# An encoder layer on one core: another order of loads and products at the beginning, another ending of the last norm

## The chip, the core and the metric

The kernel runs on one core of one Trainium2 chip. A core has a matrix engine (TensorE, PE in the profile, with its weight loads shown apart as PEld), a vector engine (VectorE, DVE), an activation engine (ScalarE, ACT), a general engine (GpSimd, POOL) and an engine that does little but issue transfers (SyncE, SP). Each works through its own list of instructions in order; semaphores tie the lists together. Data moves between the main memory and the core's own memory (128 partitions) in DMA transfers, which an engine issues and 16 DMA engines carry out. The metric is the device time of one execution in microseconds, the median over runs; lower is better.

## The reference

One layer of an encoder over 256 positions of width 2048, all in float32. Each of its three parts is normed before and after, and added to the running X:

```python
ff = swiglu(rms_norm(x, pre_norm_ffn1[layer]), w_ffn1_gate_up[layer], w_ffn1_down[layer])
x = x + 0.5 * rms_norm(ff, post_norm_ffn1[layer])
h = rms_norm(x, pre_norm_mix[layer])
...
x = x + rms_norm(mixed, post_norm_mix[layer])
ff = swiglu(rms_norm(x, pre_norm_ffn2[layer]), w_ffn2_gate_up[layer], w_ffn2_down[layer])
x = x + 0.5 * rms_norm(ff, post_norm_ffn2[layer])
```

`rms_norm` divides a row by the root of its mean square plus 1e-6 and multiplies by a gain. `swiglu` multiplies by a gate-and-up matrix of 2048 x 11264, takes silu of the gate half times the up half, and multiplies by a down matrix of 5632 x 2048. The change touches only the first products of the first `swiglu` and the last two lines of arithmetic of the whole layer.

## The kernel before

**Precision.** A float32 product is made of three products of a faster format: each operand is split into a high part `h` and a rest `l`, and `three` (L435) adds `xh*h`, `xh*l` and `xl*h` into a bank of PSUM, the matrix engine's accumulators. For weights, `split_act` (L175) makes the parts: ACT copies raw weights into `h` (a cast, L176), then DVE subtracts (`l`, L177). For X, PE transposes blocks of 128 x 128 into a bank (`turn`, L205; the operation itself is L210), ACT scales them by the norm's gain into the high part (`take_hi`, L224, L227), and DVE makes the rest (`take_lo`, L229, L232). The norm's own factor is applied later.

**Tiles.** X stands as two row tiles (m = 0, 1) of 128 rows. Its 2048 columns are 16 blocks of 128 (index k of the products), or four quarters q of 512. The gate-and-up matrix is worked in groups of 512 columns of gate and 512 of up (n = 0, 1), so a group has four banks (m, n). A pair u is two blocks of 128 rows of the weights, so a pair's raw tile holds four parts of 256 KB (k = 0, 1; n = 0, 1) and gives 24 products into the four banks. `gated.piece(u, k, m)` (L969) is six of them.

**The beginning** (L96 to L135 and L1241 to L1317). SP issues the loads in program order: first the norm's gains as 16 rows (in `to_columns`, L109, which turns them into columns with one transpose and a DVE copy), then X's first quarter of row tile 0 (`load_x`, L92, L94), the first quarter of pair 0's weights (`arrive`, L1257), X's first quarter of row tile 1, three more parts of pair 0, the second quarters of X, pair 1, the rest of X in two loads, pair 2. `busy(n)` (L126) issues n products of zeros into an unused bank; they stand in PE's list five after the start, two after the gains, three after the first transposes. Then the order is written out by hand, engine by engine (`tc.manual_schedule`, L1244): each engine carries out what stands in the code in the order in which it stands there. `half(i)` splits a part of pair 0, `taken` is the scaling and rest of transposed blocks, `square_x` (L246) is ACT's sum of squares of a quarter of X for the norm, and `split` (L158) splits the two halves of a pair's weights, ACT's cast and DVE's subtract for each half. Behind line 1317 come pairs 3 to 7 of the group, with an order that the framework chooses.

**The end** (`finish`, L686, the branch from L732). The last two pairs of the down matrix are held back, and their products are ordered bank by bank: (0,0), (0,1), (1,0), (1,1). After each bank ACT takes the sum of squares (`squares`, L712; L667), one of four columns per row tile. After a tile's second bank, `rsqrt_of` (L180) adds the four columns (L182, DVE), scales and adds eps (L184, DVE), and raises to the power -1/2 (L186, POOL). Then DVE updates X by quarters (`update`, L719, L721), the first quarter of row tile 1 goes over ACT (L727) and POOL (L728) (`update_aside`), and SP stores each quarter (`store`, L733, L735), the one that POOL makes last.

## Time and profile before

| | us |
|---|---|
| median of 3 runs | 1833.32 (1832.61 to 1833.54) |
| the profiled execution's own time | 1832.88 |
| its span, first to last instruction | 1831.1 |
| PE busy in the span | 1814.2 |
| DVE busy | 1627.3 |
| ACT busy | 1129.4 |

The granted clock was 0.997 on average. In the profile, L with a number is a line of the kernel, `out<-in` names the tiles written and read, and an arrow in brackets names what ended an engine's idle time. A timeline's row gives start and duration in us; rows that follow one another with the same form are merged, with their count after the x. In a table of windows each row gives a stretch, its length, and for each engine the busy time with the number of instructions, then the granted clock, the share of the DMA engines' time that is busy, and GB/s. Rows with "min/median/max" give durations in ns, and "DMA to landing" the us from a transfer's issue until its data has arrived.

### The profile page before, as it was taken

What the parts mean: (1) busy time and instruction counts of PE and PEld (TensorE: products, weight loads), DVE (VectorE), ACT (ScalarE), POOL (GpSimd) and SP (SyncE); (2) the same over time, 40 slices, a digit from 0 to 9 for tenths busy, and PEclk for the clock granted to TensorE, in tenths of its full rate; (3) what the DMA queues carried; (4) which work ended last, traced back from release to release, by engine and by line L of the source; (5) the groups of instructions that cost most, each with busy time, mean ns of one, the idle gap of its engine ahead of it and who ended that gap; (6) DMA issues with size and microseconds to landing.
All of it is one profiled execution on the core that took longest, in us unless ns stands there. A gap on an engine that the chain in (4) does not pass through costs nothing.

```text
span 1831.1 us, 23305 instructions
## 1 busy us (share of the span) xinstructions
PE 1814.2 (99%) x8438; PEld 1504.0 (82%) x8438; DVE 1627.3 (89%) x2071; ACT 1129.4 (62%) x1492; POOL 114.4 (6%) x115
## 2 busy tenths in 40 slices
PE   9999999999999999999999999999999999999998
PEld 6888888888887888888888888788888888888886
DVE  7999999999999998477787798899999999999897
ACT  7565666665655666476587556556666666565563
POOL 1011111111000000000000000001111111000000
PEclk9999999999999999999999999999999999999999
DMA  8789999998665566555454456789998998855565
GB/s 301 230 234 283 278 280 253 251 266 241 249 226 197 195 253 216 203 175 178 165 173 150 161 208 249 223 243 267 280 277 267 252 251 251 268 218 207 193 231 185
DMA packets 200020, 422.42 MB, mean 231 GB/s; under 512 B 10984, under 2 KB 45888, under 8 KB 199136
## 3 DMA queue, kind: packets, MB, share of 16 engines
q1 hardware_dynamic: 178880, 380.95, 59.6%
q0 software_dynamic: 21024, 39.99, 12.7%
q8 instruction: 66, 1.08, 0.2%
q14 instruction: 50, 0.41, 0.1%
HBM read 408.29 MB, written 12.60 MB: 230 GB/s over the span
## 4 chain that ended last, share of the span: by engine, by line
PE 87%; DVE 5%; ACT 3%; DMA 3%; issue 2%; POOL 0%; SPq 0%; DVEq 0%; ACTq 0%; POOLq 0%
PE pa L441 37%; PE pb L441 33%; PE pa L309 5%; DVE l L177 3%; PE pa L314 3%; DMA raw<-in_w_ffn_gate_up_dram 2%; PE pa L364 2%; PE pa L362 2%; PE pa L363 2%; ACT h L176 1%; PE pa L1074 1%; PE pb L1074 1%; PE pb L1582 0%; PE pb L1556 0%; PE pb L1660 0%
## 5 line engine op out<-in xcount | busy, mean ns | idle before, releaser
L176 ACT CAST h<-raw 128x1024 fp32r<-128x1024 f32 (+1 forms) x861 | 846.9, 1013 | 448.6 <-PE pb L441 131.9
L177 DVE TENSOR_TENSOR l<-raw,h 128x1024 fp32r<-128x1024 f32 (+1 forms) x861 | 983.1, 1171 | 118.3 <-ACT h L176 83.8
L441 PE MATMUL pa<-h,xt 128*128 128x512 f32 x1104 | 387.2, 392 | 0.1
L441 PE MATMUL pb<-h,xt 128*128 128x512 f32 x952 | 339.7, 391 | 0.4 <-DVE pb L1126 0.4
L441 PEld LDWEIGHTS pa<-h,xt 128*128 128x128 f32 x1104 | 207.2, 188 | 43.9 <-DVE xt L232 0.6
L441 PE MATMUL pa<-l,xt 128*128 128x512 f32 x552 | 215.7, 391 | 0.2 <-DVE l L177 0.2
L441 PEld LDWEIGHTS pb<-h,xt 128*128 128x128 f32 x952 | 178.6, 188 | 43.2 <-DVE pb L1133 3.5
L441 PE MATMUL pb<-l,xt 128*128 128x512 f32 x476 | 185.6, 390 | 0.0
L441 PE MATMUL pb<-h,ht 128*128 128x512 f32 x464 | 163.8, 390 | 0.0
L441 PE MATMUL pa<-h,ht 128*128 128x512 f32 x464 | 163.7, 391 | 0.0
L910 POOL DMA_DIRECT2D raw<-in_w_ffn_gate_up_dram x76 | 92.0, 1211 | 737.0 <-DVE l L177 638.8
L309 PE MATMUL pa<-xt,h 128*128 128x512 f32 x512 | 124.5, 393 | 0.2 <-ACT h L176 0.2
L441 PEld LDWEIGHTS pa<-l,xt 128*128 128x128 f32 x552 | 103.7, 188 | 21.4 <-DVE l L177 1.4
L309 PEld LDWEIGHTS pa<-xt,h 128*128 128x128 f32 x512 | 93.8, 188 | 18.6 <-ACT h L176 0.6
L441 PE MATMUL pa<-h,xs 128*128 128x512 f32 x304 | 108.5, 389 | 0.0
L441 PE MATMUL pb<-h,xs 128*128 128x512 f32 x304 | 105.9, 389 | 0.0
L441 PEld LDWEIGHTS pb<-l,xt 128*128 128x128 f32 x476 | 89.4, 188 | 17.2
L441 PEld LDWEIGHTS pa<-h,ht 128*128 128x128 f32 x464 | 87.7, 189 | 18.4
L441 PEld LDWEIGHTS pb<-h,ht 128*128 128x128 f32 x464 | 87.3, 188 | 18.1
L441 PE MATMUL pa<-l,ht 128*128 128x512 f32 x232 | 90.9, 392 | 0.0
L441 PE MATMUL pb<-l,ht 128*128 128x512 f32 x232 | 90.5, 390 | 0.0
L314 PE MATMUL pa<-xt,l 128*128 128x256 f32 x512 | 69.1, 285 | 0.0
(289 smaller groups left out, 2516.9 us busy)
## 6 DMA issues: line engine op xcount, KB each, us to landing
raw<-in_w_ffn_gate_up_dram SPq DMA_DIRECT2D x350, 512.0 KB, 6.1
raw<-in_w_ffn_down_dram SPq DMA_DIRECT2D x88, 1024.0 KB, 5.3
raw<-in_w_mix_in_dram SPq DMA_DIRECT2D x52, 1024.0 KB, 4.9
raw<-in_w_ffn_gate_up_dram POOLq DMA_DIRECT2D x76, 512.0 KB, 8.8
raw<-in_w_mix_out_dram SPq DMA_DIRECT2D x16, 1024.0 KB, 5.0
away<-ht SPq DMA_DIRECT2D x16, 512.0 KB, 6.9
ht<-away SPq DMA_DIRECT2D x16, 512.0 KB, 7.8
pg<-in_post_norm_ffn_dram SPq DMA_DIRECT2D x4, 512.0 KB, 6.7
```

The lines of the kernel that those rows point to most:

```text
L176: nc.scalar.copy(hi, src)
L177: nc.vector.tensor_tensor(lo, src, hi.bitcast(F32), ALU.subtract)
L309: nc.tensor.matmul(slot[f], weights(hs, kk, f), xcol(xt, k), start=(k == 0), stop=(k == KT - 1))
L314: nc.tensor.matmul(slot[f][:, 0:T], weights(ls, kk, f), xcol(xt, kh * 8 + kk, 0), start=False, stop=False,)
L362: nc.tensor.matmul(dst, xh, h[:, o : o + n], start=(k == 0), stop=False)
L363: nc.tensor.matmul(dst, xh, l[:, o : o + n], start=False, stop=False)
L364: nc.tensor.matmul(dst, xl, h[:, o : o + n], start=False, stop=(k == KT - 1))
L441: nc.tensor.matmul(self.bank(at), lhs, rhs, start=(n == 1), stop=n in (ends, self.of[at]), skip_group_check=n > ends,)
L910: nc.gpsimd.dma_start(raw[:, 0:1024].rearrange("p (k c) -> p k c", k=2), self.source(u, g)[:, :, 1], accum_op=ALU.add,)
L1074: nc.tensor.transpose(bank[:, o : o + P], zs[m][:, k * P : (k + 1) * P], ident)
```

## The change

At the beginning, X's first quarter is loaded in three parts (one block, one block, two blocks of 128 columns) for each row tile; the very first block is the first thing that SP issues. The gains and the first block of row tile 1 are issued from ACT. The second weight part is loaded ahead of X's next blocks, and X's other quarters follow pair 1 and pair 2 instead of standing ahead of them. `turn` can now transpose single blocks into a bank that is already in use. Pair 0's products are made block by block, and within a block the products with the weights' rest come last. The idle products are five, two and two. Transposes of blocks 1, 2 and 3 stand between pair 0's products, and those of the second quarter between the halves of pair 1. Each engine's list follows the new order, as before.

At the end, the first three of row tile 1's square sums are added, scaled and joined with eps on DVE while the last bank's products run (`rsqrt_most`), and the fourth is scaled and added afterwards (`rsqrt_rest`), in place of a reduction over four. The last store is issued from ACT.

```diff
@@ -89,10 +89,15 @@
 
     res = {"X": new_X()}
 
-    def load_x(m, q, n=1):
-        sl = slice(q * 512, (q + n) * 512)
-        nc.sync.dma_start(res["X"][:, m, sl], x[0, m * P : (m + 1) * P, sl])
-
+    def load_x(m, a, b, queue=nc.sync):
+        sl = slice(a * P, b * P)
+        queue.dma_start(res["X"][:, m, sl], x[0, m * P : (m + 1) * P, sl])
+
+    load_x(0, 0, 1)
+    stat = ctx.enter_context(tc.tile_pool(name="stat", bufs=4))
+    gain_rows = stat.tile([P, P], F32, tag="dg", name=nm("rows"), bufs=1)
+    nc.scalar.dma_start(gain_rows[:KT, :], pre_norm_ffn1[0].rearrange("(j p) -> j p", p=P))
+    load_x(1, 0, 1, nc.scalar)
     warm = const.tile([P, 4], F32, tag="warm", name="warm")
     nc.vector.memset(warm, 0.0)
     nc.scalar.activation(warm, warm, AF.Silu)
@@ -102,14 +107,15 @@
     nc.vector.memset(ones, 1.0)
     mhalf = const.tile([P, 4], F32, tag="mhalf", name="mhalf")
     nc.vector.memset(mhalf, -0.5)
-    stat = ctx.enter_context(tc.tile_pool(name="stat", bufs=4))
-
     stat.tile([P, 104], F32, tag="line", name="line", bufs=1)
 
-    def to_columns(srcs, tag, eng):
-
-        rows = stat.tile([P, P], F32, tag="dg", name=nm("rows"), bufs=1)
+    def to_columns(srcs, tag, eng, rows=None):
+
         r0 = 0
+        if rows is not None:
+            r0, srcs = srcs, ()
+        else:
+            rows = stat.tile([P, P], F32, tag="dg", name=nm("rows"), bufs=1)
         for src in srcs:
             n = src.shape[0] // P
             eng.dma_start(rows[r0 : r0 + n, :], src.rearrange("(j p) -> j p", p=P))
@@ -130,9 +136,7 @@
             nc.tensor.matmul(bank, idle[:, 0:P], idle, start=(i == 0), stop=(i == n - 1))
 
     busy(5)
-    gain1 = to_columns([pre_norm_ffn1[0]], "gain1", nc.sync)
-    load_x(0, 0)
-    busy(2)
+    gain1 = to_columns(KT, "gain1", None, gain_rows)
 
     R = const.tile([P, T], F32, tag="R", name="R")
     scales = const.tile([P, 8], F32, tag="scales", name="scales")
@@ -186,6 +190,19 @@
         nc.gpsimd.tensor_tensor(r, v, mhalf[:, 0:1], ALU.pow)
         return r
 
+    def rsqrt_most(ssq, scale, eps):
+        tot = stat.tile([P, 1], F32, tag="tot", name=nm("tot"))
+        nc.vector.tensor_reduce(tot, ssq, axis=AX.X, op=ALU.add)
+        nc.vector.tensor_scalar(tot, tot, scale, eps, ALU.mult, ALU.add)
+        return tot
+
+    def rsqrt_rest(ssq, scale, most):
+        v = stat.tile([P, 1], F32, tag="v", name=nm("v"))
+        nc.vector.tensor_scalar(v, ssq, scale, most, ALU.mult, ALU.add)
+        r = stat.tile([P, 1], F32, tag="r", name=nm("r"))
+        nc.gpsimd.tensor_tensor(r, v, mhalf[:, 0:1], ALU.pow)
+        return r
+
     far = {}
     shim = ctx.enter_context(tc.tile_pool(name="shim", bufs=1, side="right"))
     shim.tile([P, 104], F32, tag="shim", name="shim")
@@ -202,10 +219,10 @@
         open_far(2)
         return [far["pool"].tile([P, 8, 2, T], F32R, tag="xt", name=nm("xt")) for _ in range(2)]
 
-    def turn(m, q):
-
-        bank = pa() if m == 0 else pb()
-        for j in range(4):
+    def turn(m, q, bank=None, js=range(4)):
+
+        bank = bank or (pa() if m == 0 else pb())
+        for j in js:
             k = q * 4 + j
             nc.tensor.transpose(
                 bank[:, j * P : (j + 1) * P], res["X"][:, m, k * P : (k + 1) * P], ident
@@ -434,18 +451,21 @@
 
         def three(self, at, ah, al, h, l):
             for lhs, rhs in ((ah, h), (ah, l), (al, h)):
-                n = self.seen.get(at, 0) + 1
-                self.seen[at] = n
-
-                ends = self.of[at] - (self.rest if at[0] == "c" else 0)
-                nc.tensor.matmul(
-                    self.bank(at),
-                    lhs,
-                    rhs,
-                    start=(n == 1),
-                    stop=n in (ends, self.of[at]),
-                    skip_group_check=n > ends,
-                )
+                self.one(at, lhs, rhs)
+
+        def one(self, at, lhs, rhs):
+            n = self.seen.get(at, 0) + 1
+            self.seen[at] = n
+
+            ends = self.of[at] - (self.rest if at[0] == "c" else 0)
+            nc.tensor.matmul(
+                self.bank(at),
+                lhs,
+                rhs,
+                start=(n == 1),
+                stop=n in (ends, self.of[at]),
+                skip_group_check=n > ends,
+            )
 
         def plain(self, u, hs, ls, m, n, k):
             a = self.tiles[u]
@@ -700,7 +720,7 @@
             X = res["X"]
             if lead:
                 lead.load()
-            r = [None, None]
+            r, most = [None, None], [None, None]
             y = self.y
 
             def products(m, n, part):
@@ -711,8 +731,15 @@
 
             def squares(m, n):
                 self.squares(m, n)
-                if n == 1:
-                    r[m] = rsqrt_of(self.ssq[m], 1.0 / (D * mul * mul), EPS / (mul * mul))
+                if n == 1 and most[m] is None:
+                    r[m] = rsqrt_of(self.ssq[m], scale, eps)
+                elif n == 1:
+                    r[m] = rsqrt_rest(self.ssq[m][:, 3:4], scale, most[m])
+
+            scale, eps = 1.0 / (D * mul * mul), EPS / (mul * mul)
+
+            def mostly(m):
+                most[m] = rsqrt_most(self.ssq[m][:, 0:3], scale, eps)
 
             gains = self.gains
 
@@ -730,9 +757,9 @@
             ordered = {mybir.EngineType.PE, mybir.EngineType.DVE, mybir.EngineType.Activation}
             every = slice(None)
             if gain is None:
-                def store(m, q):
+                def store(m, q, queue=nc.sync):
                     sl = slice(q * 512, (q + 1) * 512)
-                    nc.sync.dma_start(out[0, m * P : (m + 1) * P, sl], X[:, m, sl])
+                    queue.dma_start(out[0, m * P : (m + 1) * P, sl], X[:, m, sl])
 
                 def in_place(n):
                     gains(1, n, dst=self.c[1][n])
@@ -749,6 +776,7 @@
                     squares(1, 0)
                     for q in range(4):
                         update(0, q)
+                    mostly(1)
                     in_place(0)
                     products(1, 1, every)
                     squares(1, 1)
@@ -759,7 +787,7 @@
                     for q in (1, 2, 3):
                         update(1, q)
                         store(1, q)
-                    store(1, 0)
+                    store(1, 0, nc.scalar)
                 return None
 
             xt = new_xt()
@@ -1244,8 +1272,8 @@
     with tc.manual_schedule():
         banks = {}
 
-        def turned(*at):
-            banks[at] = turn(*at)
+        def turned(m, q, js=range(4)):
+            banks[m, q] = turn(m, q, banks.get((m, q)), js)
 
         def taken(m, q, js=range(4)):
             take(m, q, gain1, xt, banks[m, q], js)
@@ -1257,54 +1285,84 @@
         def arrive(i):
             nc.sync.dma_start(raw[:, i * 512 : (i + 1) * 512], first[:, i // 2, i % 2])
 
-        h, l = (
-            p.tile([P, 1024], F32R, tag=t, name=nm(t)) for p, t in ((hip, "h"), (lop, "l"))
+        hs, ls = zip(
+            *(
+                [p.tile([P, 1024], F32R, tag=t, name=nm(t)) for p, t in ((hip, "h"), (lop, "l"))]
+                for _ in range(2)
+            )
         )
+        gated.parts = {0: (hs, ls)}
 
         def half(i):
-            cs = slice(i * 512, (i + 1) * 512)
-            split_act(h[:, cs], l[:, cs], raw[:, cs])
-
-        def piece(m, n):
-            gated.plain(0, [h], [l], m, n, 0)
+            cs = slice(i % 2 * 512, (i % 2 + 1) * 512)
+            split_act(hs[i // 2][:, cs], ls[i // 2][:, cs], raw[:, i * 512 : (i + 1) * 512])
+
+        def piece(k, m, n, order):
+            a, ms, cs = gated.tiles[0], slice(m * P, (m + 1) * P), slice(n * 512, (n + 1) * 512)
+            terms = (0, hs), (0, ls), (1, hs)
+            for i, w in (terms[j] for j in order):
+                gated.one(("c", m, n), a[:, k, i, ms], w[k][:, cs])
+
+        def block(k, n):
+            for m in range(2):
+                piece(k, m, n, (0, 2))
+            for m in range(2):
+                piece(k, m, n, (1,))
+
+        def column(j):
+            for m in range(2):
+                turned(m, 0, [j])
+
+        def column_taken(j):
+            for m in range(2):
+                taken(m, 0, [j])
 
         arrive(0)
-        load_x(1, 0)
         arrive(1)
+        load_x(0, 1, 2)
+        load_x(1, 1, 2)
         arrive(2)
         arrive(3)
-        load_x(0, 1)
-        load_x(1, 1)
+        load_x(0, 2, 4)
+        load_x(1, 2, 4)
         raws = [load(gated.source(1))]
-        load_x(0, 2, 2)
-        load_x(1, 2, 2)
+        load_x(0, 4, 8)
+        load_x(1, 4, 8)
         raws.append(load(gated.source(2)))
-        turned(0, 0)
+        load_x(0, 8, 16)
+        load_x(1, 8, 16)
+        turned(0, 0, [0])
         taken(0, 0, [0])
-        busy(3)
         half(0)
-        taken(0, 0, [1, 2, 3])
-        turned(1, 0)
-        piece(0, 0)
+        busy(2)
+        turned(1, 0, [0])
+        busy(2)
+        piece(0, 0, 0, (0, 2))
         taken(1, 0, [0])
         half(1)
-        piece(1, 0)
-        piece(0, 1)
-        piece(1, 1)
-        hs, ls = zip((h, l), split_half(raw, 1))
-        gated.parts = {0: (hs, ls)}
-        taken(1, 0, [1, 2, 3])
-        gated.piece(0, 1, 0)
-        gated.piece(0, 1, 1)
+        piece(0, 1, 0, (0, 2))
+        for m in range(2):
+            piece(0, m, 0, (1,))
+        column(1)
+        column_taken(1)
+        block(0, 1)
+        half(2)
+        half(3)
+        block(1, 0)
+        column(2)
+        column(3)
+        block(1, 1)
+        column_taken(2)
+        column_taken(3)
         gated.parts[1] = split(raws[0])
+        for m in range(2):
+            gated.piece(1, 0, m)
+        for m in range(2):
+            turned(m, 1)
+            taken(m, 1)
         square_x(0, 0)
-        turned(0, 1)
-        turned(1, 1)
-        taken(0, 1)
-        taken(1, 1)
-        for k in range(2):
-            for m in range(2):
-                gated.piece(1, k, m)
+        for m in range(2):
+            gated.piece(1, 1, m)
         gated.parts[2] = split(raws[1])
         square_x(1, 0)
         for k in range(2):
```

## The prediction

> **What bounds the kernel now.** I read the page's first part, then the timeline of the first 30 us, then TensorE's (PE's) products by window, then the chain of waits and the DMA shares at the end.
>
> ```profile
> span 1831.1 us, 23305 instructions
> PE 1814.2 (99%) x8438; PEld 1504.0 (82%) x8438; DVE 1627.3 (89%) x2071; ACT 1129.4 (62%) x1492; POOL 114.4 (6%) x115
> ```
>
> PE is busy for all but 17 us, and from its first real product to its last it works almost without a gap. So a change of the two ends can only move where that stretch starts, what it loses on the way, and what follows its end. The start, from the timeline (start, duration, engine, line; in brackets the idle time and who ended it):
>
> ```profile
> 0.73 1.28 ACT L98 ACT_TABLE_LOAD   x1 [0.73 <-PEq L1846]
> 0.74 0.40 SPq L115 DMA_DIRECT2D rows<-in_pre_norm_ffn_dram  x1
> 1.20 0.41 SPq L94 DMA_DIRECT2D X<-in_x_dram  x1
> 1.37 2.31 PE L130 MATMUL pb<-idle 128*128 128x512 bf16 x5 [1.37 <-DVE idle L124]
> 3.94 0.17 DVE L120 COPY gain<-pb 128x16 f32<-128x16 f32 x1 [2.62 <-PE pb L119]
> 5.05 0.73 PE L210 MATMUL pa<-ident,X 128*128 128x128 f32 x4 [0.18 <-DMA X<-in_x_dram]
> 5.62 0.81 PE L130 MATMUL pb<-idle 128*128 128x512 bf16 x3
> 6.11 0.62 ACT L176 CAST h<-raw 128x512 fp32r<-128x512 f32 x1
> 6.22 0.35 DVE L232 SCALAR_TENSOR_TENSOR xt<-pa,gain,xt 128x128 fp32r<-128x128 f32 x1 [2.10 <-ACT xt L227]
> 6.76 0.69 DVE L177 TENSOR_TENSOR l<-raw,h 128x512 fp32r<-128x512 f32 x1 [0.19 <-ACT h L176]
> 6.90 0.63 PE L210 MATMUL pb<-ident,X 128*128 128x128 f32 x4 [0.47 <-DMA X<-in_x_dram]
> 7.28 0.47 PE L441 MATMUL pa<-h,xt 128*128 128x512 f32 x1
> ...
> 11.91 1.05 ACT L176 CAST h<-raw 128x1024 fp32r<-128x1024 f32 x1 [1.23 <-DMA raw<-in_w_ffn_gate_up_dram]
> 13.26 1.05 ACT L176 CAST h<-raw 128x1024 fp32r<-128x1024 f32 x1 [0.30 <-DMA raw<-in_w_ffn_gate_up_dram]
> 13.86 0.60 PE L210 MATMUL pa<-ident,X 128*128 128x128 f32 x4
> 14.22 0.62 ACT L254 ACTIVATE jk<-X 128x512 bf16<-128x512 f32 x1
> 14.84 1.12 ACT L227 ACTIVATE xt<-pa,gain 128x128 fp32r<-128x128 f32 x4
> 15.84 1.16 ACT L227 ACTIVATE xt<-pb,gain 128x128 fp32r<-128x128 f32 x4
> 18.30 1.23 DVE L177 TENSOR_TENSOR l<-raw,h 128x1024 fp32r<-128x1024 f32 x1
> ```
>
> X's first 256 KB, issued at 1.20, reach PE at 5.05; the first weight block is cast at 6.11; the second 256 KB of X let PE go on at 6.90; the first product starts at **7.28**. Later weights come at one rate: 11.91 and 13.26, two 512 KB halves 1.35 us apart, so 0.67 us for 256 KB. How smoothly PE then runs:
>
> ```profile
> core 0: us, PE busy (x) PEld busy (x), PEclk, DMA share, GB/s
> 14.65:20.19 5.54, 5.54 (x25) 4.59 (x26) 1.00 1.04 386
> 7.28:13.86 6.58, 6.34 (x24) 4.09 (x24) 1.00 1.04 397
> ```
>
> Pair 1's 24 products take 5.54 us (0.23 each, no gap); pair 0's 24 take 6.58, so waits cost **1.06 us** there. The end:
>
> ```profile
> 1823.31 0.16 DVE L182 TENSOR_REDUCE tot<-ssqr 128x1 f32<-128x4 f32 x1 [0.99 <-ACT jk L667]
> 1823.50 0.15 DVE L184 TENSOR_SCALAR v<-tot 128x1 f32<-128x1 f32 x1
> ```
> ```profile
> 1826.00:1826.50 0.50, 0.00 (x0) 0.00 (x0) 0.45 (x1) 0.00 (x0) 0.44 (x1) 0.50 0.97 369
> 1826.50:1827.00 0.50, 0.00 (x0) 0.00 (x0) 0.00 (x0) 0.00 (x0) 0.00 (x0) 0.50 1.06 385
> 1827.00:1827.50 0.50, 0.00 (x0) 0.00 (x0) 0.00 (x0) 0.00 (x0) 0.00 (x0) 0.50 1.11 361
> ```
>
> The reduction of the square sums is a 0.19 us step after the last square (1823.31 to 1823.50), and DVE stood idle for 0.99 us ahead of it. The last four stores then keep the DMA engines full (the last column but one, the DMA share, is 0.97 to 1.11).
>
> **The start, step by step.** *First product.* X's first block (64 KB) takes the issue slot at 0.74, and the first weights (256 KB) the one at 1.20 that X's 256 KB had. The startup is slow, then full:
>
> ```profile
> 4.00:4.50 0.50, 0.50 (x2) 0.00 (x0) 0.12 (x1) 0.00 (x0) 0.00 (x0) 1.00 0.20 66
> 5.00:5.50 0.50, 0.45 (x3) 0.45 (x4) 0.00 (x0) 0.00 (x0) 0.00 (x0) 1.00 1.05 402
> ```
>
> I let the weights inherit that slot's landing, 5.0. The cast (0.62) then ends at 5.65 and the first product starts at **5.70**: -1.58 us. X's side is earlier: gain is there at 4.11, transpose, scaling (0.37: four in 1.12, 0.25 apart) and residual (0.35, the row at 6.22) end near 4.95. Bounds: weights landing before 4.4 help no more (X's side and the idle products in front then set 5.2); at worst they land as now, at 6.1.
>
> *Moved to ACT's queue.* The trace has no DMA issued from ACT; at SP's 0.40 each, both issues end by 1.6, table load (1.28) and warm-up by 3.1, and ACT's first scaling comes after 4.11: hidden. If the table load goes first, the gains are issued at 2.0 and land (1.5 us, below) at 3.5, still under the idle products, which end at 3.68. X's second block lands 1.5 to 3.8 us after an issue at 1.2, 2.7 to 5.0; I take 5.0.
>
> ```profile
> DMA to landing us min/median/max: 1.5/1.5/1.5
> DMA to landing us min/median/max: 3.8/5.9/8.4
> ```
>
> (The gains' rows, then X's loads.) SP has nine issues before pair 1's weights, as now, so nothing queued on it starts later. A 64 KB block costs between 0.17 us (by bytes) and 0.67 (as many packets as 256 KB); I take 0.25. At either end pair 1's weights land at 10.0 to 11.5, before ACT wants them at 11.9.
>
> The Trainium skill speaks against small blocks: "DMA: Bandwidth & Descriptors", section "Rules for kernel authors", says that transfers under 64 KB are mostly overhead, and its section on measured bandwidth gives 0.95 us for 64 KB. By that, an estimate, pair 0's third weight block lands 1.4 us later and the sum rises by about 0.2.
>
> *Pair 0.* The removed idle products stood in waits and count nothing. Of the eight transposes of X's first quarter, six now stand behind the first product: 6 x 0.11 (four in 0.60, one lasting 0.27) = **+0.65**. Its waits: row 1's residual must follow the first subtract on DVE (5.68 to 6.28, then 0.35), so PE waits 0.3 at 6.4; I find no other over 0.1. So 1.06 becomes 0.3: **-0.75**.
>
> *Pair 1.* PE's new order is: transposes of columns 2 and 3, six products, then pair 1. ACT's is: four scalings of those columns, **then** the cast of pair 1's weights, and DVE's subtract follows the cast. From the start of the transposes: 0.31 until the first is read, 1.04 for four scalings (14.84 to 15.84 is four), 1.05 cast, 1.23 subtract, with 0.09 of hand-overs 3.72 until PE can take pair 1's second product. PE is there after 0.44 + 6 x 0.23 + 0.23 = 2.03. **+1.69**, all idle. Before, those weights were cast at 11.91, while PE still had pair 0 to do.
>
> *Pair 2.* The second quarter's eight transposes now stand between pair 1's halves, so PE has 12 products ahead of pair 2, not 24. ACT: four transposes 0.64, eight scalings 2.02, a square 0.62 (14.22 to 14.84), cast 1.05; DVE 1.23; hand-overs 0.08: 5.64. PE: 0.87 + 12 x 0.23 + 0.23 = 3.83. **+1.81**. With 24 products PE needed 6.6, which covered it: that cover is what the change takes away. After pair 2, each pair gives PE 5.5 us against ACT's 2.1 and DVE's 2.4, so the delay stays and doesn't grow.
>
> Start: -1.58 + 0.65 - 0.75 + 1.69 + 1.81 = **+1.8 us** (+1.3 with first weights by 4.4, +2.9 with 6.1).
>
> **The end.** The total of three sums moves under the wait for the fourth (DVE idle until 1823.31): two small instructions, 0.35 us, hidden by DVE's 0.99 us of idle time; uncovered they would cost that 0.35. The chain loses 0.19 and its scale-and-add gets an operand from memory:
>
> ```profile
> L1682 DVE TENSOR_SCALAR mx<-mx,sink x8: 220/222/231, 837.6 to 1023.0; 128x2 f32<-128x2 f32 x8
> ```
> ```profile
> 1826.48 0.83 SPq L735 DMA_DIRECT2D out_dram<-X  x2
> ```
>
> 0.22 against the 0.15 of the row at 1823.50, so +0.07: net -0.12. The last store, second of the two issues from 1826.48, can go out up to 0.4 earlier from ACT, but the DMA engines are full: between 0 and -0.4, nearer the full engines, -0.1. End: **-0.2** (-0.1 to -0.5).
>
> **Sum.** +1.6 us on the profiled execution's 1832.9 gives 1834.5; the median shown lies 0.4 above that execution; I say **1834.7**.
>
> **Rivals.**
> 1. *The two new waits don't come* (ACT casts pair 1's and pair 2's weights ahead of the scalings). For: ACT is idle for over a us at 11.91 now. Against: in the timeline ACT's square, scalings and casts stand in the written order. 1.8 - 3.5 - 0.2 = -1.9: **1831.3**, faster but within 0.2%.
> 2. *The first weights come no earlier*: the slow startup belongs to the moment (66 GB/s at 4.0 to 4.5), not to the slot, or the block on ACT's queue is late. Products then start near 6.8: +1.1 to +1.4, **1836**.
> 3. *The other side: PE stays at half rate.* Five idle products in 2.31 us are 0.43 apart, the three at 5.62 are 0.22 apart, though the granted clock reads 1.00: PE's rate doubles between. The change takes away five idle products and puts four back, and PE idles more before 5.7. At half rate a product costs 0.2 more; from ten such products on the kernel is slower by over 0.2%; all of pair 0 so would be 4.5 more, **1839**. Against it: the five idle products from 1.37 stay. The Trainium skill, "TensorE: Matmul & The Clock Gate", section "Part 1: The HAM clock gate", has the array at half clock until about 3.4 us of steady work in a free-running window; the trace agrees (rate doubled 2.9 to 4.2 us after 1.37), and by that rule the gate opens in time unless the new gaps break the window.
>
> **How the numbers follow.** Forecast 0.60, rival 1 0.18, rival 2 0.14, rival 3 0.08. About 0.2% (3.7 us) is what a measurement of this kernel can tell from no change. The forecast and rival 1 lie within it, rival 2 nearly all, rival 3 mostly outside. Faster by over 0.2% needs more than rival 1, with a shift in the freely scheduled middle: 0.05. Slower: 0.12, same: 0.83. The likeliest alone spans 1833.8 to 1836 (the bounds of landing and end); down to rival 1's upper half and up past rival 2 the range is **1831.6 to 1836.8**.
>
> **What would show it.** Right: a first product near 5.7; PE idle 0.7 and 1.0 us before pair 1's first two products, and again at pair 2, ended by ACT's cast and DVE's subtract; reduce gone from the end's chain. Wrong: no such idle time, a first product after 6.5, or products 0.43 apart after it.

## The result, and the profile after

The changed kernel takes **1838.45 us** (median of 8 runs, 1836.79 to 1841.08) against 1833.93 for the kernel before in the same comparison (8 runs, 1830.65 to 1835.99): a ratio of **1.0025, 95% interval 1.0014 to 1.0036**. It is slower by some 4.5 us, outside the range of the prediction. The profiled execution took 1838.56 us, its span is 1836.8.

The first part of the page of the changed kernel:

```profile
span 1836.8 us, 23311 instructions
PE 1815.1 (99%) x8437; PEld 1504.9 (82%) x8437; DVE 1628.4 (89%) x2073; ACT 1129.5 (61%) x1493; POOL 114.3 (6%) x115
```

The span has grown by 5.7 us and PE's busy time by 0.9: nearly all of it is time in which PE waits. The start, from the timeline of the changed kernel (start, duration, engine, line; in brackets the idle time and who ended it):

```profile
5.67 1.41 PE L461 MATMUL pa<-h,xt 128*128 128x512 f32 x2
6.88 0.80 PE L461 MATMUL pb<-h,xt 128*128 128x512 f32 x2
7.51 0.39 PE L461 MATMUL pa<-l,xt 128*128 128x512 f32 x1
...
11.49 0.37 ACT L244 ACTIVATE xt<-pa,gain 128x128 fp32r<-128x128 f32 x1 [1.56 <-PE pa L227]
12.56 0.40 PE L461 MATMUL pb<-l,xt 128*128 128x512 f32 x1
12.81 1.98 ACT L180 CAST h<-raw 128x1024 fp32r<-128x1024 f32 x2
13.89 0.50 PE L461 MATMUL pa<-h,xt 128*128 128x512 f32 x1 [0.93 <-ACT h L180]
15.15 0.50 PE L461 MATMUL pa<-l,xt 128*128 128x512 f32 x1 [0.76 <-DVE l L181]
...
22.22 0.51 PE L461 MATMUL pa<-h,xt 128*128 128x512 f32 x1 [0.64 <-ACT h L180]
23.48 0.50 PE L461 MATMUL pa<-l,xt 128*128 128x512 f32 x1 [0.76 <-DVE l L181]
```

The first product starts at 5.67 instead of 7.28. Then the four waits stand that the new order was to bring, at pairs 1 and 2, ended by ACT's cast and DVE's subtract. The brackets count from a modelled end that lies 0.17 us behind the next possible start (0.40 against a spacing of 0.23), so I count what a wait costs from start to start, less 0.23: 13.89 follows a product of 12.56, so 1.10; 15.15 follows 13.89, so 1.03; 2.13 us at pair 1. At pair 2 (a product at 21.19, then 22.22 and 23.48) it is 0.80 and 1.03, 1.83 us. At pair 2's second product the changed kernel is 3.1 us behind the kernel before.

So far this is what the prediction had, a little larger. What it had not comes 20 us later. The same view of both kernels; first the changed one:

```profile
13.29 0.61 SPq L928 DMA_DIRECT2D raw<-in_w_ffn_gate_up_dram  x1
...
17.50 2.99 SPq L928 DMA_DIRECT2D raw<-in_w_ffn_gate_up_dram  x3
24.59 1.20 SPq L156 DMA_DIRECT2D raw<-in_w_ffn_gate_up_dram  x2
34.01 1.05 ACT L180 CAST h<-raw 128x1024 fp32r<-128x1024 f32 x1 [3.39 <-DMA raw<-in_w_ffn_gate_up_dram]
43.06 0.55 POOL L190 TENSOR_TENSOR r<-v,mhalf 128x1 f32<-128x1 f32 x1 [1.96 <-DVE v L188]
44.38 0.49 PE L295 MATMUL pb<-dg,ones 128*128 128x128 f32 x2 [2.62 <-DVE dg L294]
```

Then the kernel before:

```profile
16.84 0.61 SPq L900 DMA_DIRECT2D raw<-in_w_ffn_gate_up_dram  x1
20.95 1.20 SPq L152 DMA_DIRECT2D raw<-in_w_ffn_gate_up_dram  x2
27.75 1.05 ACT L176 CAST h<-raw 128x1024 fp32r<-128x1024 f32 x1
38.41 0.38 PE L278 MATMUL pb<-dg,ones 128*128 128x128 f32 x2
```

Read it downwards. Pair 5's weights (issued at 24.59 instead of 20.95) need the buffer that pair 2's last subtract gives back, and this subtract is late by the two waits. In the meantime SP's list sends four halves of a later group's preload (L928: one at 13.29, three from 17.50) ahead of pair 5, where the list of before had one, and since SP's loads land in the order of their issue (in all profiles here, over the first 50 us), pair 5's first half lands at 33.91 instead of 27.65. ACT's list has the cast of pair 5 ahead of the squares of X: it stands for 3.39 us. The norm's factor comes out of the squares, and PE's two products that spread it (L295) start at 44.38 after **2.78 us** of idle time, where PE before came to the first of them without any.

And then the granted clock falls. Windows of the changed kernel, then of the kernel before (length, PE busy with its products, granted clock, DMA):

```profile
41.35:44.76 3.41, 0.79 (x5) 1.00 0.83 282
44.76:48.17 3.41, 3.41 (x11) 0.50 0.44 135
48.17:51.58 3.41, 3.41 (x17) 1.00 0.59 210
```
```profile
558.20:561.61 3.41, 1.37 (x6) 1.00 0.00 0
561.61:565.03 3.42, 3.42 (x10) 0.50 0.90 316
```

The counts in these rows also take in products that lie across an edge of the window and small ones of the spread, so the price is read from the spacing. Timeline of the changed kernel, from the last part of the stretch into the window behind it:

```profile
47.59 0.63 PE L461 MATMUL pa<-h,xt 128*128 128x512 f32 x1
48.02 0.47 PE L461 MATMUL pb<-h,xt 128*128 128x512 f32 x1
48.33 0.40 PE L461 MATMUL pb<-l,xt 128*128 128x512 f32 x1
48.56 0.63 PE L461 MATMUL pb<-h,xt 128*128 128x512 f32 x2
```

A product costs 0.43 us there (47.59 to 48.02) and 0.23 behind it (48.33 to 48.56). In 3.41 us that is 8 products instead of 15: 7 x 0.23 = **1.6 us**. The kernel before has such a stretch too, at 561.61 after a wait of its own (10 products in 3.87 us instead of 2.27), which the changed kernel's profile doesn't have. So the changed kernel, 7.4 us behind at 49 us, is 6.2 us behind at the last product.

The end: the reduction is out of the chain, and one store goes from ACT. Timeline of the changed kernel, then its DMA issues of the end (how many, KB each, median us from issue to landing):

```profile
1827.79 0.15 DVE L195 TENSOR_REDUCE tot<-ssqr 128x1 f32<-128x3 f32 x1
1829.48 0.21 DVE L201 TENSOR_SCALAR v<-ssqr,tot 128x1 f32<-128x1 f32 x1 [0.74 <-ACT jk L687]
```
```profile
out_dram<-X SPq DMA_DIRECT2D x7, 256.0 KB, 2.7
out_dram<-X ACTq DMA_DIRECT2D x1, 256.0 KB, 3.2
```

From the last product's start to the end of the span it is 8.51 us (9.00 before).

### The profile page after: what moved, and what is told of

It is laid out like the page before. It is cut to its first block, busy times and chain, and to the rows that moved or that the text cites. A ratio compares the mean times of both kernels' runs of the same rounds, so it can differ in the third digit from the quotient of the medians.

```text
span 1836.8 us, 23311 instructions
## 1 busy us (share of the span) xinstructions
PE 1815.1 (99%) x8437; PEld 1504.9 (82%) x8437; DVE 1628.4 (89%) x2073; ACT 1129.5 (61%) x1493; POOL 114.3 (6%) x115
## 3 DMA queue, kind: packets, MB, share of 16 engines
q8 instruction: 66, 1.08, 0.2%
## 4 chain that ended last, share of the span: by engine, by line
PE 77%; DVE 10%; DMA 5%; ACT 3%; issue 2%; SPq 0%; POOL 0%; DVEq 0%; ACTq 0%; POOLq 0%
PE pa L461 32%; PE pb L461 28%; DVE l L181 5%; PE pa L326 5%; DMA raw<-in_w_ffn_down_dram 3%; PE pa L331 3%; PE pa L381 2%; PE pa L379 2%; PE pa L380 2%; DMA raw<-in_w_ffn_gate_up_dram 2%; ACT h L180 2%; DVE raw L493 1%; DMA X<-in_x_dram 1%; DVE sp L181 1%; PE pa L1102 0%
```

## Experiments

Ratios are to runs of the kernel before on the same chip; a ratio and its interval come from all runs of both, so it isn't quite the quotient of the medians. The median of the kernel before was 1831.97 us (33 runs) beside experiments 1 (first set), 3, 4 and 6, 1831.82 (22) beside 2, 7 and 10, 1832.46 (27) beside 1 (second set), 5 and 8, and 1832.22 (9) beside 9. "Idle" is counted as above, from start to start less 0.23.

**1. The end alone** (kernel before, with the end's edits: `rsqrt_most`, `rsqrt_rest`, last store from ACT).

> The kernel before with the change's end alone (square sums added ahead, last store from ScalarE). The prediction's term: 0.2 us less than before (0.1 to 0.5). In the changed kernel's profile the time from the last product's start to the span's end is 8.5 us against 9.0 before, so theory A (the end brings what the changed profile shows) expects 0.4 to 0.5 less there, theory B (full DMA engines make the other queue worthless) 0.1 to 0.2. Both lie below what the times can tell; the profile decides. Start and middle as before.

1831.17 us, 0.9990 (0.9981 to 0.9999). A second set of runs of the same kernel, to see whether that was chance:

> The kernel before with the end's change alone, once more, beside the same runs of before as the two casts. If the end is worth 0.2 to 0.8 us: ratio 0.9990 to 0.9999, as the first time (0.9990, 0.9981 to 0.9999). If the first was chance: 0.9995 to 1.0010.

1831.62 us, 0.9994 (0.9985 to 1.0003). From the last product to the end of the span: 8.81 and 8.75 us, against 9.00 before. The end is worth 0.2 us in the trace and 0.8 in both medians; only the first interval leaves out 1.

**2. The beginning alone** (changed kernel, its end as before).

> The changed kernel without its end (the end's code as before). If the loss is all the beginning's and the end gains 0.3 to 0.8 us by itself: 5 us over before, 1837 beside a before of 1832 (1.0024 to 1.0032), with PE's waits at pairs 1 and 2 and at the norm's spread (2 to 3 us) as in the changed kernel. Rival, that the two parts hinder each other: within 0.1% of before.

1837.46 us, 1.0033 (1.0021 to 1.0046). The waits are the same three (2.1, 1.8 and 2.4 us idle), with a half-rate stretch behind the third. All of the loss is the beginning's. With its end undone the last product stands 8.77 us from the end, 8.51 with it: again 0.25 for the end. (That the changed beginning by itself shortens this by 0.24 I can't explain.)

**3. Preloads held back** behind pair 5's weights in SP's list:

```
+            with tc.issue_after(pair5) if aside else ExitStack():
+                gated.plan()
-            gated.plan()
```

(`pair5` is the issue of pair 5's last load, noted beside.)

> The changed kernel, with the preloads of the next column group (line 928) kept behind the loads of pair 5 in SyncE's list; nothing else. Theory A (the 3 us wait of TensorE at 44.4 us comes from pair 5's weights, which land at 33.9 because four preloads of 512 KB were put ahead of them in SyncE's list, so that ScalarE's list stands still from 30.6 to 34.0 in front of the square sums): the first half of pair 5 lands near 28 to 29, ScalarE does not wait, TensorE's wait at the norm's spread falls from 2.8 us to under 0.5, the half-rate stretch at 44.8 to 48.2 goes, together about 4 us less than the changed kernel: 1834 to 1835. Theory B (ScalarE and VectorE are simply 3 us behind since pair 2, whatever is loaded when): the wait stays at 2 to 3 us and the time at 1838. The waits at pairs 1 and 2 (2.1 and 1.8 us) stay by both.

1835.3 us, 1.0016 (1.0007 to 1.0025). The waits at pairs 1 and 2 stay at 2.1 and 1.8. Timeline of this kernel:

```profile
24.58 1.50 SPq L158 DMA_DIRECT2D raw<-in_w_ffn_gate_up_dram  x2
43.28 0.49 PE L297 MATMUL pb<-dg,ones 128*128 128x128 f32 x2 [0.82 <-DVE dg L296]
```

Pair 5 goes out at the same moment but lands at 28.53, the idle time at the spread falls from 2.78 to 0.99, and no half-rate stretch follows. Behind the spread this kernel is 3.8 us behind the kernel before, where the changed kernel is 7.4. The queue ahead of pair 5 is one link of the loss. (The two intervals of the ratio overlap; the place of the change is plain in the trace, its size in the median is not.)

**4. Casts first**: the first cast of pairs 1 and 2 ahead of the scalings.

```
         block(1, 1)
+        early = [split_half(raws[0], 0)]
         column_taken(2)
         column_taken(3)
-        gated.parts[1] = split(raws[0])
+        early.append(split_half(raws[0], 1))
+        gated.parts[1] = tuple(zip(*early))
```

(and the same for pair 2, ahead of the second quarter's transposes.)

> The changed kernel, with the first half of pair 1's and of pair 2's weights cast and subtracted ahead of the scalings that stood before them; nothing else written by hand (the framework's list for SyncE changes with it: two preloads of 512 KB instead of four stand ahead of pair 5). By the prediction's reasons the two waits go: pair 1's from 2.1 to under 1.0, pair 2's from 1.8 to 0.3 or less, about 2.5 to 3 us. If the late second half of pair 2 is also what delays pair 5's load (its buffer is freed by that subtract), the wait at the spread shrinks too, and the whole is 5 to 6 us less than the changed kernel: 1832 to 1833. If the waits at pairs 1 and 2 have another cause, nothing changes.

1831.4 us, 1.0001 (0.9992 to 1.0010): the loss is gone. Timeline of this kernel:

```profile
11.36 1.05 ACT L180 CAST h<-raw 128x1024 fp32r<-128x1024 f32 x1 [1.45 <-DMA raw<-in_w_ffn_gate_up_dram]
13.71 0.50 PE L461 MATMUL pa<-l,xt 128*128 128x512 f32 x1 [0.49 <-DVE l L181]
22.03 1.20 SPq L156 DMA_DIRECT2D raw<-in_w_ffn_gate_up_dram  x2
39.96 0.49 PE L295 MATMUL pb<-dg,ones 128*128 128x128 f32 x2 [0.44 <-DVE dg L294]
```

The cast now starts as soon as the weights land. Pair 1 costs 0.70 us instead of 2.13, pair 2 nothing, the spread 0.60, and no stretch before the last product is at half rate. The order of these casts is the root. With it SP's list changes too, which the framework makes: two preload halves instead of four stand ahead of pair 5 here. So this edit loosens two links of the chain at once and doesn't say what each weighs.

**5. Each cast by itself.**

> The changed kernel with the first cast of pair 1's weights alone put ahead of the four scalings; pair 2 stays as changed. If each of the two waits carries through: pair 1's wait falls from 2.1 to 0.7 us, pair 2's stays near 1.8 us, pair 5's load is issued 1 us or so earlier (near 23.5) and lands late still, PE waits at the spread 1 to 2.5 us: 1.0010 to 1.0022 of before, about half of what both casts bring. If pair 1's wait is only handed on to pair 2: pair 2's wait grows by 1 us or more and the time is that of the changed kernel, 1.0025 to 1.003.

1835.2 us, 1.0013 (1.0004 to 1.0022). Pair 1's wait is 0.75, pair 2's stays at 1.83; pair 5 is issued at 23.39, and the spread costs 0.26, less than expected.

> The changed kernel with the first cast of pair 2's weights alone put ahead of the second quarter's scalings; pair 1 stays as changed. If pair 2's subtract decides when pair 5's load goes out: no wait at pair 2, pair 5 issued near 23.3, a wait at the spread under 1.5 us, no half-rate stretch: 1.0005 to 1.0015 of before. If the two waits only add up as PE's idle time: 1.8 us less than the changed kernel, 1.0015 to 1.002.

1834.16 us, 1.0007 (0.9998 to 1.0016). No wait at pair 2, pair 1's 2.1 stays, pair 5 is issued at 23.34, the spread costs 0.99. Each cast brings a part of the loss back, and neither wait is handed on to the other.

**6. Both repairs** (3 and 4 together).

> The changed kernel with both edits: casts ahead of the scalings, and preloads behind pair 5's loads. If both causes hold, no wait over 1 us is left before 100 us, first product near 5.7, and the time is below the kernel before: 1830 to 1833. If the spread's wait has another cause it is still there, 1834 to 1836.

1832.06 us, 1.0003 (0.9994 to 1.0012): with the casts first, holding the preloads adds nothing. No wait of over 1 us was expected to be left, but the spread costs 1.19 in this profile, and pair 1 1.45 in two waits.

**7. Squares earlier**: the six later squares written ahead of the last quarter's scalings, so that they stand ahead of pair 5's cast.

```
-        for q in (2, 3):
-            for m in range(2):
-                taken(m, q)
+        for m in range(2):
+            taken(m, 2)
+        for m in range(2):
+            for q in (1, 2, 3):
+                square_x(m, q)
+        for m in range(2):
+            taken(m, 3)
```

> The changed kernel, but with the six later squares of X written into the hand order ahead of the scalings of X's last quarter, so that they stand on ACT ahead of the cast of pair 5, whose weights land late. If that place in ACT's list is what makes the norm's spread late: the wait of 2.8 us there falls under 0.5 us and the half-rate products after it (1.3 us) go, while the waits at pairs 1 and 2 stay: 3.5 to 4 us less than the changed kernel, a ratio of 1.000 to 1.001. If the late weights themselves hold PE, the wait moves to pair 5's or pair 6's products and the ratio stays at 1.002 or more.

> Casts of pairs 1 and 2 ahead of the scalings, and the six later squares ahead of the last quarter's scalings: both repairs in one. If the waits add up, the remaining wait at the spread (0.6 us) and the one behind it (0.65 us) go: 1830.5, about 1 us under the casts alone, ratio 0.9993. If the squares now delay the last quarter's scalings, PE waits before pair 6: no faster than the casts alone (1.0001).

Both missed: 1837.1 us, 1.0030 (1.0018 to 1.0041), and with the casts first 1833.21, 1.0007 (0.9998 to 1.0016). In the first, only two of the six squares came ahead of the cast of pair 5 in ACT's list. The norm's second factor was there 4.1 us earlier (39.54 instead of 43.65), and yet PE waited 2.49 us. Timeline of this kernel:

```profile
41.68 0.22 DVE L285 TENSOR_SCALAR scales<-scales 128x2 int32<-128x2 int32 x2
42.95 0.28 DVE L294 TENSOR_SCALAR dg<-ident,scales 128x128 f32<-128x128 f32 x1
43.28 0.80 PE L295 MATMUL pb<-dg,ones 128*128 128x128 f32 x2 [2.33 <-DVE dg L294]
```

The residuals of the last quarter, pushed back by the squares, now stand ahead of the factor's last steps in DVE's list: between 39.6 and 41.7 DVE does those, then one subtract. In the second kernel two subtracts stand there. The edit moved the wait from one engine's list to another's, and it doesn't tell whether the late weights would have held PE anyway.

**8. Idle products in the wait**: 16 products of ones by ones ahead of the spread, to keep PE busy.

> The changed kernel with 16 idle products (ones by ones, 128x128, 0.11 us each, 1.8 us in all) in PE's list just ahead of the norm's spread, into unused columns of its bank. If PE's idle time there closes the clock gate: the idle stretch before the spread falls from 2.8 to about 1 us, the products after it come 0.23 us apart instead of 0.43, and the time is about 1.3 us under the changed kernel beside it, 1.0017 to 1.0025 of before, although PE has more to do. If the half rate has another cause: products still 0.43 apart for 3.4 us after the spread, and no gain.

1843.84 us, 1.0052 (1.0039 to 1.0066). Also a miss, twice over. They took 3.5 us, not 1.8 (32 records of 0.11), and the other work was arranged anew around them. Timeline of this kernel:

```profile
44.87 0.39 PE L299 MATMUL pb<-dg,ones 128*128 128x128 f32 x2
49.83 0.69 DVE L181 TENSOR_TENSOR l<-raw,h 128x512 fp32r<-128x512 f32 x1 [3.45 <-ACT h L180]
50.78 0.65 PE L299 MATMUL pb<-dg,ones 128*128 128x128 f32 x2 [4.59 <-DVE dg L298]
```

The first product of the spread comes without a wait and no half-rate stretch starts at it, as was expected if idle time closes the clock's gate. But the second product's operand now stands in DVE's list behind a subtract of a preload that lands late, and PE waits 4.75 us there; the half-rate stretch comes behind this wait, from 50.97.

**9. The spread later**: the two products one pair later in PE's list (and the in-place products with them); loads and casts up to there as in the changed kernel.

```
-                if u == 4:
+                if u == 5:
                     power_and_rest()
                     spread(two)
-                for done in {4: (0, 1, 2), 5: (3, 4), ...
+                for done in {5: (0, 1, 2, 3, 4), ...
```

> The changed kernel with the norm's spread (and the five in-place products with it) one pair of weights later in the program; the loads and casts up to there keep their order. If the late norm alone holds PE there, and the clock halves only because of it: the waits at pairs 1 and 2 stay (2.1 and 1.8 us), the 2.8 us before the spread fall under 0.5, no products 0.43 us apart after it, and the time is 3 to 4 us under the changed kernel: 1.0003 to 1.0010 of before. If the late weights themselves hold PE: pair 5's or pair 6's products wait as long in its place, and the time stays at 1.002 to 1.003.

> The same with the casts of pairs 1 and 2 ahead of the scalings. If a wait of 0.6 us at the spread and one of 0.65 us behind it were all that was left: about 1 us under the casts alone, 0.9993 to 1.0000 of before. If putting the spread later makes the in-place products late for the next group: a new wait after 48 us, and 1.0005 or more.

1848.0 us, 1.0081 (1.0067 to 1.0094), and with the casts first 1842.39, 1.0052 (1.0040 to 1.0065): far slower, but the first answers the question. Windows of that kernel, then its timeline:

```profile
15.70:19.11 3.41, 3.41 (x11) 0.50 1.03 402
24.80:48.00 23.20, 23.20 (x111) 1.00 0.67 232
```
```profile
66.88 0.80 PE L461 MATMUL pa<-l,xt 128*128 128x512 f32 x1 [3.58 <-DVE l L181]
```

From pair 2's last wait to 48.00 PE is busy without a gap, through the whole of pair 5, although pair 5's weights land at 32.99, nearly as late as in the changed kernel (33.91). So **late weights by themselves hold nothing up; the late norm does**. (In the changed kernel itself the subtract of pair 5's first half ends at 38.39, and PE is through with pair 4 only at 41.61.) The spread still costs 1.08 us here, at 50.30, not under 0.5. What it then costs to put it later is other waits: the in-place products crowd DVE's list from 51 us on, and a subtract behind them holds PE for 3.7 us at 66.88. Four half-rate stretches (from 15.70, 66.90, 572.07 and 1193.30) take about 1.6 us each on top. With the casts first the same wait came, 3.9 us at 62.97, as the second branch of its expectation had it.

**10. The loads alone**: order and end as in experiment 1, but the gains and X's second 256 KB issued on ACT, X's first 256 KB in SP's first slot.

> The kernel before with its end changed, its hand order kept, and only the loads moved: the gains and X's second 256 KB issued on ACT, X's first 256 KB in SP's first slot, the first weights in the second. If the order costs and the loads alone gain: first product at 6.1 to 6.6 (7.28 before), no new waits at pairs 1 and 2, a time 0.7 to 1.1 us under that of the changed end alone, ratio 0.9983 to 0.9990. Rival, that the clock gate decides the start (PE reaches full rate at 5 or at 7 us by chance of phase): first product early but products 0.43 us apart after it, and a ratio of 0.999 to 1.0.

1832.32 us, 1.0004 (0.9995 to 1.0013). The first product came at 8.56 us, **later** than before. Timeline, then DMA issues:

```profile
4.70 0.26 PE L125 MATMUL pb<-ident,rows 16*128 16x16 f32 x1 [1.01 <-DMA rows<-in_pre_norm_ffn_dram]
8.56 0.63 PE L459 MATMUL pa<-h,xt 128*128 128x512 f32 x1
```
```profile
rows<-in_pre_norm_ffn_dram ACTq DMA_DIRECT2D x1, 8.0 KB, 3.8
```

The 8 KB of gains, issued at 0.73 beside 256 KB of X, took 3.8 us; beside a 64 KB block, in the changed kernel, 2.0. And though the products start 1.1 us after those of the first run of experiment 1, the last product starts at 1821.41, 0.24 us *earlier* than there (1821.65). Product by product, the two profiles show where the lead went. At pair 1's first product 0.68 us of it are left, because pair 0 took 0.45 us less in the later kernel. At 555 us it is still there, 0.96 us, and at 571 us it is gone. Timeline of experiment 1's kernel (first run), then of the loads-alone kernel:

```profile
558.42 2.94 ACT L176 CAST h<-raw 128x1024 fp32r<-128x1024 f32 x3 [0.49 <-DVE raw L492]
559.52 0.50 PE L454 MATMUL pb<-h,sp 128*128 128x512 f32 x1 [1.11 <-ACT h L176]
```
```profile
558.28 2.95 ACT L181 CAST h<-raw 128x1024 fp32r<-128x1024 f32 x3 [0.37 <-DVE raw L497]
558.98 0.91 PE L459 MATMUL pb<-h,sp 128*128 128x512 f32 x2
```

The cast that PE needs there starts at 558.42 and 558.28, whichever way PE comes to it: the kernel that leads waits 1.27 us for it (from a product at 558.02), the other 0.18. The second profile of experiment 1 does the same (first product at 8.37, 1.05 behind the first profile at 555 us, last product at 1821.22). In these profiles **the moment of the first product doesn't set the end**: the lead was kept for 550 us and lost in one wait.

## Why the prediction was wrong

*First product:* 5.70 foreseen, 5.67 measured. *X and gains on ACT's queue:* landing at 4.72 (5.0 taken) and 2.75 (3.5), hidden as said, so rival 2 fell; ACT's issues took 0.42 and 0.44. *Pair 1's weights:* 11.29 landed, foreseen 10.0 to 11.5. The small blocks cost nothing visible: two of 64 KB landed 0.19 and 0.17 us behind their neighbours, the price by bytes.

*Pair 0* came out otherwise in this profile: -0.75 taken. From 5.67 to 12.79 it takes 7.12 us, less 0.65 for the six transposes 6.47, against 6.58 before: **-0.1**. The difference is rival 3 in small. The first products stand 0.79, 0.43 and 0.39 apart, as the idle ones do, because PE reached its full rate at 7.21 us, in the profile of before at 5.25. The rule that I cited (the Trainium skill, "TensorE: Matmul & The Clock Gate", "Part 1: The HAM clock gate") has a window that runs free of the kernel, and the trace agrees: over all profiles the rate doubled anywhere from 5.2 to 8.9 us. I priced that rival from ten products on; it came as some four. And it came by chance: in experiment 6 and in the first kernels of 7 and 9, whose products up to the end of pair 0 stand in the same order, the full rate began at 5.55, 5.56 and 5.46, and by the same count pair 0 took 5.7 to 5.8 us, **-0.8**. The term was right where the clock opens early.

*Pair 1:* +1.69 foreseen, 2.13 measured; the first scaling started 0.52 us after the first transpose rather than 0.31, and four scalings took 1.32 us rather than 1.04 because one waited for DVE. *Pair 2:* +1.81 foreseen, 1.83 measured. Right in kind and nearly in size; rival 1 fell.

**The step that failed** is the sentence after it: "After pair 2, each pair gives PE 5.5 us against ACT's 2.1 and DVE's 2.4, so the delay stays and doesn't grow." It asks whether ACT and DVE keep up with PE, and they do: experiment 9 has PE busy without a gap for 23 us. It doesn't ask what else hangs on the subtract that had become late. That subtract frees a weight buffer, the buffer lets pair 5's load out, the load queues behind four preload halves, ACT's list stands at its cast, and the norm behind it reaches PE 2.78 us late, with a half-rate stretch of 1.6 us after that. The prediction followed SP's list up to pair 1's weights only; behind line 1317 the framework makes that list, and it changed with the edit, from one preload half ahead of pair 5 to four. Experiments 3 and 4 loosen links of this chain, and the wait at the spread shrinks to 0.99 and 0.60 with no half rate behind it; 9 shows that the norm, not the weights, is the link that PE feels. The count, against the +1.8 us foreseen for the start: +3.1 at pair 2's second product (0.65 of the excess from pair 0, 0.44 from pair 1), +4.3 more by this chain up to 49 us, less 1.2 in the middle: +6.2 at the last product. In the middle 0.6 goes at the wait at 558 us, which is shorter in the changed kernel, and 1.6 by the half-rate stretch at 561 us that only this profile of the kernel before has; later waits give 1.0 back. Whether a half-rate stretch comes hangs also on where the clock's windows fall (last section), which differs from execution to execution: +6.2 is one draw, and the medians of the two kernels are 4.5 apart.

*The end:* -0.2 foreseen; 0.20, 0.25 and 0.25 measured in the three pairs of profiles that differ in it alone. Of the ACT-issued store I said that the full engines hide most of its gain; it took 3.2 us to land, SP's 2.7. In the last addition 1834.5 and 0.4 give 1834.9, not the 1834.7 that was said; this is small beside the miss.

The signs "right" that the prediction named all came true, and of those for "wrong" only the products 0.43 us apart. Signs that cover the foreseen steps alone can't show a missing one.

## What to carry to other kernels

Where an edit delays the last reader of a rotating buffer, follow the buffer: to the load that waits for it, to what stands ahead of that load in its queue, to the engine whose ordered list stands at its cast, and to everything behind it there. Cast new weights ahead of the scalings in an engine's list when the next consumer of the weights is nearer. An earlier first product is worth nothing by itself where a later wait ends at a moment that doesn't move with it; look for such waits through the whole trace, here one at 558 us, before you count the gain.

## What the runs showed of the hardware

In these profiles PE's clock, up to the last product, falls to half for exactly one window of 3.41 us at a time, and the windows form a grid that starts anywhere and then holds for the whole execution. In the changed kernel the full rate starts at 7.21 and ends at 44.76: 37.55 us, 11 windows of 3.413. In the kernel before, 5.25 to 561.62 is 163 of them. On that grid, PE's idle time in the window ahead decides. Worked out from the sixteen profiles, all windows with over 1.9 us idle that run at full rate, without the one that holds the last product (a product counts 0.23 us, a transpose 0.11, a product 256 wide 0.12, and what is left is idle; a few hundredths hang on these three):

```
idle us in the window -> clock in the next
1.92  1.93  1.94  1.94  1.95  1.96  1.97  1.97  2.00  2.03   full
2.04  2.19  2.20  2.21  2.26  2.31  2.39  2.41  2.44  2.45
2.54  2.70  2.88  3.30  3.39                                 half
```

The edge lies at 2.0 to 2.2 us, some 60% of a window. That is why the changed kernel's 2.13 us at pair 1 cost no clock (1.10 in one window, 1.03 in the next), while a like wait in experiment 9's first kernel, at another phase, lay in one window (2.20) and brought half rate (its row at 15.70, products 0.43 apart). The Trainium skill, "TensorE: Matmul & The Clock Gate", has the window and its free running in "Part 1: The HAM clock gate", and the traces agree; in "Why this matters for your kernels" it advises against gaps of over about 3 us, and there the measurement differs: 2.2 us in one window, in two pieces, were enough.

That the phase also makes the runs of one kernel differ by a few us fits the mean clock on record for every run, but isn't proven by it. One half-rate stretch takes 0.0009 off that mean (half of 3.41 us in 1831). Of the 91 runs of the kernel before beside the experiments, the 44 with a mean of 0.999 have a median of 1831.89 us, the 38 with 0.998 1832.74, and the 9 with 0.997 1835.14. All eight runs of the changed kernel are at 0.998 or below.
